# A three-layer network in one program: modulation through the attention, other banks, later norm rows, earlier decays

## The chip, the cores and the metric

One core of a Trainium2 chip runs the whole program. The metric is the device time of one execution, in microseconds (us). The kernel before was timed three times: the median is 1394.43 us, the lowest 1393.12 and the highest 1401.13. A further execution was recorded by the profiler.

## The reference, cut to what matters

The input is 256 tokens of width 1024, in float32. Two blocks follow each other. The first is a dilated window attention over three groups of eight heads, beside a pooling branch:

```python
h = rmsnorm(x, norm_g) * (1 + scale) + shift            # from c @ w_ada
q, k, v, z, u, ... = h @ w_in                           # 3 groups x 8 heads x 64
logits = q k^T / 8 + bias ; attn = softmax-merge of the 3 groups
merged = sigmoid(g_attn) * ((attn * silu(z_attn)) @ w_attn_br) \
       + sigmoid(g_pool) * ((pool(u) * silu(z_pool)) @ w_pool_br)
x = rmsnorm(x + gate * (merged @ w_out), final_g)
```

The second has two layers, on the 256 tokens `x` and on 256 context tokens `xc`. Each layer gets six vectors from `silu(c) @ w_mod` and six from `silu(c_ctx) @ w_mod`:

```python
sh1, sc1, g1, sh2, sc2, g2 = modulation(c, w_mod[i], b_mod[i])
h = x * (1 + sc1) + sh1                                 # the same for xc
y = mixer(h) @ w_out     # layer 0: retention (decay log1p(-exp(theta))) and gated linear
                         # attention (GLA), heads normalised; layer 1: window attention
x = layer_norm(alpha * x + g1 * y) * ln_g + ln_b
x = layer_norm(alpha * x + g2 * (relu(h2 @ w1)**2 @ w2)) * ln_g + ln_b
```

## The kernel before, in words

Every large product is made from float32 operands that are split into a rounded high part and the rest. `mm3` (L162) issues three matmuls for each tile: high by high, high by rest, rest by high. A weight tile of 512 KB is loaded by a DMA on SyncE's queue (`wload`, L135, four buffers `raw`), rounded by ScalarE (`whi`, L141) and subtracted by VectorE (`wlo`, L142). An activation is split in the same way by `split` (L108 to L111, tiles like `fx`).

PSUM has eight banks (L105): three named `mm` for the large products, two `S` for attention scores, two `T` for transposes, and one `O`. A tile that asks for a bank waits until the readers of its last holder are done.

The order of each engine's instructions is made when the program is built, by a scheduler that simulates the engines. `tc.issue_after(x)` holds back what is issued in it until the instruction x is placed. Each engine then runs its list strictly in order.

The first stage (0 to 54 us) makes the first block's shift and scale. Then come the products with `w_in` (54 to 217 us), the first block's attention (217 to 274), pooling and merging (274 to 360), `w_out` and the final norm (360 to 385), the modulation of the second block's first layer, `modulate` (L335), and the start of its products (385 to 405), retention (405 to 495), GLA (495 to 600), `proj_out` (600 to 655), the MLP of layer 0 (655 to 1030), window attention of layer 1 (1040 to 1175), its `proj_out`, and the MLP of layer 1 (to the end).

Fillers. The six modulation vectors of layer 0 need 24 MB of `w_mod`. A generator `quad` (L235) loads them 512 KB at a time on SyncE's queue (L257, tile `mvraw`, three buffers) and multiplies each with the two conditioning vectors (L251). All the products of one `quad` add into one tile in bank `O`, which it holds from its first step to its last. `fill(n)` steps the generators n times; `fill_behind` does so after each weight load of a large product, `rate[0]` steps at a time. Layer 1's vectors are made in the MLP of layer 0 by `summed` (L275), with the multiplications on VectorE (L292, tile `mva`).

Attention of the first block. `attention(h2)` (L549) treats two heads. For each of two query halves: scores on TensorE (L567, bank `S`); on VectorE the bias tile `B` is added and a row maximum taken (L570); exponent on ScalarE (L576), one over the sum and the scaling on VectorE (L577, L578); transposes on TensorE (L201, bank `T`), copies on ScalarE (L584). Then the products with v (L590), into bank `O`. The bias tiles are loaded by DMAs on GpSimd's queue (L554, two buffers). Ahead of the four head pairs `finish()` runs the generator that is under way to its end, so that bank `O` is free; no filler runs in the four head pairs.

Ends of stages. `modulate` transposes a normed row tile, scales and shifts it on ScalarE (`hf`, L346), rounds it (`hA`, L348) and subtracts (L349) on VectorE. Around it in program order stand the multiplication of the rows `xs` by `final_g` on GpSimd (L681) and the chain of small operations on 128x8 tiles that makes the decays from `ret_theta` (L684 to L705), with `W` (L720, L721) and `decs` (L726) made from it. `gla_out` (L921) makes the GLA output of one token tile in bank `O`; `head_norm` (L729) squares it on ScalarE (`hsq`, L733), sums on VectorE (L735), takes the root on GpSimd (`rs_y`, L206) and scales on VectorE (`yg`, L740). In the MLP, `late()` runs behind the split of the first hidden tiles (`g == 0`): `new_resid` (L996) multiplies the layer norm's output `r` by the gain and adds the bias, two VectorE operations for each of four row tiles (L997, L998), which gives the residual rows (`A1t` for the context, `xs` for the tokens).

Of the kernel before, what the change touches and what calls it, by code (L numbers as in the profile page):

```python
# [95 lines left out]
def body(tc, a, cst, out):  # L96
    nc = tc.nc
    with ExitStack() as ctx:
# [7 lines left out]
        def bank(tag):  # L106
            return psum.tile([P, 512], F32, tag=tag, name=tag, bufs={"mm": 3, "S": 2, "T": 2, "O": 1}[tag])
# [11 lines left out]

        def finish():  # L120

            if fillers and fillers[0].gi_running is False and fillers[0].gi_frame is not None and fillers[0].gi_frame.f_lasti > 0:
                for _ in fillers.pop(0):
                    pass
# [212 lines left out]
        def modulate(z, cols, dst, t0):  # L337

            A, B = cols
            for c in range(0, KC, 4):  # L340
                pt = bank("T")
                hf = tmp([P, 4, P], "hf")
                for i in range(4):
                    transpose(pt[:, i * P:(i + 1) * P], z[:, (c + i) * P:(c + i + 1) * P])
                for i in range(4):
                    nc.scalar.activation(hf[:, i, :], pt[:, i * P:(i + 1) * P], AF.Identity, scale=A[:, c + i:c + i + 1], bias=B[:, c + i:c + i + 1])  # L346
                hi, lo = (t[:, c:c + 4, t0:t0 + P] for t in dst)
                nc.vector.tensor_copy(hi, hf)  # L348
                nc.vector.tensor_sub(lo, hf, hi.bitcast(F32))  # L349
# [123 lines left out]

        nc.gpsimd.memset(relb[32:33, :], 1.0)
# [75 lines left out]
        def attention(h2):  # L550
# [6 lines left out]
            for qt in range(2):  # L557
# [4 lines left out]
                for g0, g1 in parts:  # L562
# [5 lines left out]
                    for e in range(2):  # L568
                        m = small.tile([P, 1], F32, tag="m", name="m")
                        nc.vector.tensor_tensor_reduce(out=prs[e][:, g0:g1, 0:nk], in0=sv[e], in1=Bs[e][:, g0:g1, 256 - nk:256], scale=-1.0,  # L570
                                                       scalar=3.0e38 if mins[e] is None else mins[e], op0=ALU.add, op1=ALU.min, accum_out=m)
                        mins[e] = m
                for e in range(2):
# [11 lines left out]
            o = bank("O")  # L585
# [12 lines left out]
        finish()  # L598
        for h2 in range(4):
            attention(h2)  # L600

# [78 lines left out]
        for t in range(2):  # L680
            nc.gpsimd.tensor_mul(xs[:, t, :], xs[:, t, :], fg)  # L681


        th = p2r.tile([P, 8], F32, tag="th", name="th")  # L684
        nc.gpsimd.dma_start(th, bcast_rows(a["ev_ret_theta_2"].rearrange("o d h -> o (d h)")))
        e_ = p2r.tile([P, 8], F32, tag="e_", name="e_")
        nc.scalar.activation(e_, th, AF.Exp)
        w_ = p2r.tile([P, 8], F32, tag="w_", name="w_")
        nc.vector.tensor_scalar(w_, e_, -1.0, 2.0, op0=ALU.mult, op1=ALU.add)
        nc.vector.reciprocal(w_, w_)  # L690
        nc.vector.tensor_mul(w_, w_, e_)
        w2 = p2r.tile([P, 8], F32, tag="w2", name="w2")
        nc.vector.tensor_mul(w2, w_, w_)
        ser = p2r.tile([P, 8], F32, tag="ser", name="ser")
        nc.vector.tensor_scalar(ser, w2, 1.0 / 13, 1.0 / 11, op0=ALU.mult, op1=ALU.add)
        for n in (9, 7, 5, 3, 1):
            nc.vector.tensor_mul(ser, ser, w2)
            nc.vector.tensor_scalar_add(ser, ser, 1.0 / n)
        nc.vector.tensor_mul(ser, ser, w_)
        nc.vector.tensor_scalar_mul(ser, ser, -2.0)  # L700
        ln_ = p2r.tile([P, 8], F32, tag="ln_", name="ln_")
        nc.scalar.activation(ln_, e_, AF.Ln, scale=-1.0, bias=1.0)
        big = p2r.tile([P, 8], F32, tag="big", name="big")
        nc.vector.tensor_single_scalar(big, e_, 0.25, op=ALU.is_gt)
        nc.vector.copy_predicated(ser, big.bitcast(U32), ln_)  # L705
# [12 lines left out]
        W = p2r.tile([P, 4, 384], F32, tag="W", name="W")  # L718
        for h in range(4):
            nc.vector.tensor_scalar_mul(W[:, h, :], dpn[:, 1, :], lgc[:, 4 + h:5 + h])  # L720
            nc.vector.scalar_tensor_tensor(W[:, h, :], dpn[:, 0, :], lgc[:, h:h + 1], W[:, h, :], op0=ALU.mult, op1=ALU.add)  # L721
        nc.scalar.activation(W, W, AF.Exp)
        decs = p2r.tile([P, 2, 8], F32, tag="decs", name="decs")
        for i in range(2):
            for d in range(2):
                nc.vector.tensor_scalar_mul(decs[:, i, 4 * d:4 * d + 4], lgc[:, 4 * d:4 * d + 4], sdec[:, i, d:d + 1])  # L726
# [194 lines left out]
        def gla_out(T):  # L921
            o = bank("O")
# [83 lines left out]
        def mlp(layer, Ts, xks, y, pool, mid, late, norm, after):  # L1006
# [4 lines left out]
            for g in range(8):  # L1011
# [24 lines left out]
                for i in range(0 if layer and g < 1 else 2):  # L1036
                    if g:
                        ws = w_a(w1, 512 * g + 256 * i)
                    for j in range(2):
# [8 lines left out]
                        split(fh[:, 2 * i + j, :], fl[:, 2 * i + j, :], f)  # L1048
                if g == 0:
                    with tc.issue_after(queued["split"]):  # L1050
                        late()
                    rate[0] = 2
# [53 lines left out]
        def late0():  # L1106
            for T in range(4):
                new_resid(T, r0[:, T, :], lnr)
# [151 lines left out]
        def late1():  # L1260
            for T in (2, 3):
                new_resid(T, r1[:, T, :], lnr1)
# [45 lines left out]
```

## Time and profile before

| | |
|---|---|
| median of three executions | 1394.43 us |
| profiled execution, its own time | 1394.03 us |
| its span, first to last instruction | 1392.2 us |
| TensorE (PE) busy | 1306.7 us, 94% |
| VectorE (DVE) busy | 823.2 us, 59% |
| ScalarE (ACT) busy | 575.3 us, 41% |
| GpSimd (POOL) busy | 90.7 us, 7% |
| mean DMA rate | 160 GB/s |

A group of instructions has its line in the program, the engine, what it writes and reads, and how many there are. The number in square brackets of a timeline row is the time that the engine was idle just before, and what ended that. PEclk is the clock that TensorE was granted: 1.00 is 2.4 GHz, 0.50 is 1.2 GHz, and a value between is a stretch with some of both. Matmul records are gathered in the timeline: "x4" is four records, and one `mvraw` tile of 512 KB leaves four.

### The profile page before, as it was taken

Reading aid. Unit: us, or ns where it says so; the run is one execution under the profiler, and the core shown is the slowest. Engines: PE = TensorE matmul, PEld = TensorE weight load, DVE = VectorE, ACT = ScalarE, POOL = GpSimd, SP = SyncE. Lnnn points to the kernel's source line nnn. Section 1 sums busy time; section 2 is a strip of 40 time slices with the busy share of each in tenths; the row PEclk is TensorE's granted clock in tenths of the full one; section 3 lists DMA queues with packets and bytes.
Section 4 is the critical chain, followed back from the end, with each engine's and each line's share of the span. In section 5 each row is a group of like instructions: output and inputs, shape, how many; then the busy total and the mean of one; then the engine's idle time right before and its main releaser. Section 6 shows DMA issues by size and latency. Waiting matters only on the chain.

```text
span 1392.2 us, 19721 instructions
## 1 busy us (share of the span) xinstructions
PE 1306.7 (94%) x7786; PEld 1058.7 (76%) x7786; DVE 823.2 (59%) x1318; ACT 575.3 (41%) x923; POOL 90.7 (7%) x144
## 2 busy tenths in 40 slices
PE   6999998899989999898799999999989898899995
PEld 5888864469887777677777777777769776698985
DVE  3534434436763447647676656663667888656566
ACT  2533323424552254323322332233345576465652
POOL 2010021000010300101000000000011000000000
PEclk9999998899999999989989999999999999899998
DMA  9898884375532141216354566553333504365661
GB/s 331 302 299 278 282 287 138 100 248 167 173 112 76 51 121 62 102 34 206 112 158 134 174 230 196 182 184 105 91 121 104 163 16 143 109 203 173 191 178 49
DMA packets 137988, 222.22 MB, mean 160 GB/s; under 512 B 8605, under 2 KB 86053, under 8 KB 137895
## 3 DMA queue, kind: packets, MB, share of 16 engines
q1 hardware_dynamic: 131984, 206.07, 46.5%
q0 software_dynamic: 5168, 14.34, 3.5%
q8 instruction: 61, 1.00, 0.3%
q10 hardware_dynamic: 742, 0.55, 0.1%
q14 instruction: 33, 0.26, 0.1%
HBM read 217.18 MB, written 1.13 MB: 157 GB/s over the span
## 4 chain that ended last, share of the span: by engine, by line
PE 84%; DVE 7%; DMA 3%; issue 2%; ACT 2%; POOL 0%; SPq 0%; DVEq 0%; ACTq 0%; POOLq 0%
PE mm L165 23%; PE mm L166 22%; PE mm L167 22%; PE O L251 3%; PE T L201 2%; PE mm L460 1%; DMA mvraw<-in_w_mod_dram 1%; DVE wlo L142 1%; PE O L1231 1%; DMA B<-tabd 1%; PE O L590 1%; PE O L429 1%; PE S L1206 1%; PE T L790 1%; DMA h1a<-in_w_ada_dram 1%
## 5 line engine op out<-in xcount | busy, mean ns | idle before, releaser
L142 DVE TENSOR_TENSOR wlo<-raw,whi 128x1024 fp32r<-128x1024 f32 x261 | 318.5, 1223 | 241.5 <-ACT whi L141 235.5
L141 ACT CAST whi<-raw 128x1024 fp32r<-128x1024 f32 x261 | 273.5, 1051 | 429.1 <-PE mm L167 227.3
L165 PE MATMUL mm<-whi,fx 128*128 128x512 f32 x384 | 155.2, 404 | 12.7 <-DVE y L1060 9.3
L166 PE MATMUL mm<-wlo,fx 128*128 128x512 f32 x384 | 152.9, 399 | 0.0
L167 PE MATMUL mm<-whi,fx 128*128 128x512 f32 x384 | 148.4, 400 | 0.0
L165 PEld LDWEIGHTS mm<-whi,fx 128*128 128x128 f32 x384 | 73.3, 191 | 36.8 <-DVE y L1060 9.7
L165 PE MATMUL mm<-A1a,whi 128*128 128x256 f32 x352 | 101.2, 288 | 0.0
L167 PE MATMUL mm<-A1a,wlo 128*128 128x256 f32 x352 | 99.6, 283 | 0.0
L166 PE MATMUL mm<-A1a,whi 128*128 128x256 f32 x352 | 99.4, 282 | 0.0
L166 PE MATMUL mm<-hBl,whi 128*128 128x512 f32 (+1 forms) x256 | 98.4, 385 | 0.0
L167 PEld LDWEIGHTS mm<-whi,fx 128*128 128x128 f32 x384 | 73.2, 191 | 17.3
L166 PEld LDWEIGHTS mm<-wlo,fx 128*128 128x128 f32 x384 | 73.3, 191 | 16.2
L165 PEld LDWEIGHTS mm<-A1a,whi 128*128 128x128 f32 x352 | 66.2, 188 | 15.2 <-issue 12.5
L292 DVE SCALAR_TENSOR_TENSOR mva<-mvraw,cst_m,mva 128x1024 f32<-128x1024 f32 x56 | 70.7, 1279 | 0.2
L1062 DVE TENSOR_TENSOR y<-y,mm 128x512 f32<-128x512 f32 x72 | 46.9, 682 | 37.4 <-PE mm L167 37.3
L167 PEld LDWEIGHTS mm<-A1a,wlo 128*128 128x128 f32 x352 | 66.3, 188 | 3.4 <-issue 3.4
L166 PEld LDWEIGHTS mm<-A1a,whi 128*128 128x128 f32 x352 | 66.3, 188 | 2.7 <-issue 2.7
L111 DVE TENSOR_TENSOR fx<-f,fx 128x512 fp32r<-128x512 f32 (+1 forms) x60 | 34.0, 566 | 56.2 <-ACT fx L110 56.0
L166 PE MATMUL mm<-hDl,whi 128*128 128x256 f32 x224 | 63.2, 282 | 0.0
L1046 ACT ACTIVATE f<-mm 128x512 f32<-128x512 f32 (+1 forms) x58 | 28.5, 491 | 78.3 <-PE mm L167 78.3
L166 PEld LDWEIGHTS mm<-hBl,whi 128*128 128x128 f32 x256 | 49.0, 192 | 10.4 <-issue 0.4
L165 PE MATMUL mm<-whi,hA 128*128 128x512 f32 x128 | 51.3, 401 | 0.0
(501 smaller groups left out, 2862.6 us busy)
## 6 DMA issues: line engine op xcount, KB each, us to landing
raw<-in_mlp_w_dram SPq DMA_DIRECT2D x128, 512.0 KB, 4.1
mvraw<-in_w_mod_dram SPq DMA_DIRECT2D x96, 512.0 KB, 5.0
raw<-in_w_in_dram SPq DMA_DIRECT2D x64, 512.0 KB, 6.6
raw<-in_ev_w_in_dram SPq DMA_DIRECT2D x25, 512.0 KB, 4.1
raw<-in_od_w_qkv_dram SPq DMA_DIRECT2D x12, 512.0 KB, 3.6
mvraw<-in_w_ada_dram SPq DMA_DIRECT2D x10, 512.0 KB, 7.3
raw<-in_w_out_dram SPq DMA_DIRECT2D x8, 512.0 KB, 3.9
raw<-in_ev_w_out_dram SPq DMA_DIRECT2D x8, 512.0 KB, 3.8
```

The costliest lines, as they stand in the source:

```text
L111: queued["split"] = nc.vector.tensor_sub(lo, src, hi.bitcast(F32)).ins
L141: nc.scalar.copy(hi, raw)
L142: queued["lo"] = nc.vector.tensor_sub(lo, raw, hi.bitcast(F32)).ins
L165: nc.tensor.matmul(o, lh, rh, start=first, stop=False)
L166: nc.tensor.matmul(o, lh, rl, start=False, stop=False)
L167: nc.tensor.matmul(o, ll, rh, start=False, stop=last)
L201: nc.tensor.transpose(o, i, ident[:n, :n])
L251: nc.tensor.matmul(acc[32 * j:32 * j + 32, :n], stat[:, k, :], raw[:, j * n % 1024:j * n % 1024 + n], start=k == 0, stop=k == KC - 1)
L292: nc.vector.scalar_tensor_tensor(acc, raw, stat[:, k, m:m + 1], acc, op0=ALU.mult, op1=ALU.add)
L429: nc.tensor.matmul(acc[32 * j:32 * j + 32, 0:P], cst_a[:, 4 * i + k, :], rs[j // 2][:, 256 * k + P * (j % 2):256 * k + P * (j % 2) + P], s ...
L1046: nc.scalar.activation(f, o, AF.Relu)
L1062: nc.vector.tensor_add(y[:, T, hs], y[:, T, hs], o)
```

## The change

Five things are done.

1. `finish()` goes away. Each query half of the first block's attention calls `fill(3)` behind its scores, eight times in all, so that the generators of layer 0's modulation go on there. Because a `quad` holds bank `O` meanwhile, the attention's output takes a bank `mm`. After the attention `rate[0]` is 1 where it was 2.
2. `gla_out` takes bank `O` for even and bank `S` for odd token tiles.
3. The chain of decays, with its DMA of `ret_theta` and its two table functions, is issued in the first stage.
4. `xs` times `final_g` goes from GpSimd to VectorE; it, `W` and `decs` are held back until the last subtraction of `modulate` is placed.
5. In the MLP of both layers, the layer norm's rows are only copied into the residual at `g == 0`, on ScalarE. The gain and the bias follow in place, one row tile for each of `g` 2 to 5 (layer 0) or 2 and 3 (layer 1).

```diff
--- before.py
+++ after.py
@@ -117,12 +117,6 @@
-        def finish():
-
-            if fillers and fillers[0].gi_running is False and fillers[0].gi_frame is not None and fillers[0].gi_frame.f_lasti > 0:
-                for _ in fillers.pop(0):
-                    pass
...
@@ -346,7 +340,7 @@
                 nc.vector.tensor_copy(hi, hf)
-                nc.vector.tensor_sub(lo, hf, hi.bitcast(F32))
+                queued["mod"] = nc.vector.tensor_sub(lo, hf, hi.bitcast(F32)).ins
...
@@ -469,6 +463,30 @@
+        th = const.tile([P, 8], F32, tag="th", name="th")
+        nc.gpsimd.dma_start(th, bcast_rows(a["ev_ret_theta_2"].rearrange("o d h -> o (d h)")))
+        e_ = const.tile([P, 8], F32, tag="e_", name="e_")
+        nc.scalar.activation(e_, th, AF.Exp)
...
+        for n in (9, 7, 5, 3, 1):
+            nc.vector.tensor_mul(ser, ser, w2)
+            nc.vector.tensor_scalar_add(ser, ser, 1.0 / n)
...
+        nc.scalar.activation(ln_, e_, AF.Ln, scale=-1.0, bias=1.0)
...
@@ -570,6 +588,7 @@
+                fill(3)
                 for e in range(2):
                     pv = prs[e][:, :, 0:nk]
...
@@ -582,7 +601,7 @@
-            o = bank("O")
+            o = bank("mm")
...
@@ -595,9 +614,9 @@
-        finish()
         for h2 in range(4):
             attention(h2)
+        rate[0] = 1
...
@@ -677,32 +696,9 @@
-        for t in range(2):
-            nc.gpsimd.tensor_mul(xs[:, t, :], xs[:, t, :], fg)
...
-        th = p2r.tile([P, 8], F32, tag="th", name="th")
...
-        nc.scalar.activation(e_, th, AF.Exp)
...
-        nc.vector.copy_predicated(ser, big.bitcast(U32), ln_)
+        with tc.issue_after(queued["mod"]):
+            for t in range(2):
+                nc.vector.tensor_mul(xs[:, t, :], xs[:, t, :], fg)
...
+        with tc.issue_after(queued["mod"]):
+            W = p2r.tile([P, 4, 384], F32, tag="W", name="W")
...
@@ -919,7 +916,7 @@
-            o = bank("O")
+            o = bank("OS"[T % 2])
...
@@ -1046,9 +1043,9 @@
+                with tc.issue_after(queued["split"]):
+                    late(g)
                 if g == 0:
-                    with tc.issue_after(queued["split"]):
-                        late()
                     rate[0] = 2
...
@@ -1103,9 +1100,12 @@
-        def late0():
-            for T in range(4):
-                new_resid(T, r0[:, T, :], lnr)
+        def late0(g):
+            for T in range(4) if g == 0 else [g - 2] if 1 < g < 6 else []:
+                if g:
+                    new_resid(T, resid(T), lnr)
+                else:
+                    nc.scalar.copy(resid(T), r0[:, T, :])
...
@@ -1257,9 +1257,12 @@
-        def late1():
-            for T in (2, 3):
-                new_resid(T, r1[:, T, :], lnr1)
+        def late1(g):
+            for T in (2, 3) if g == 0 else [g] if g in (2, 3) else []:
+                if g:
+                    new_resid(T, resid(T), lnr1)
+                else:
+                    nc.scalar.copy(resid(T), r1[:, T, :])
```

The lines of the changed program stand six lower from L117 on, and differ more further down. The scheduler makes these orders of it.

TensorE's list in the first block's attention, in the second head pair (`S` are scores, `T` transposes, `PT,A0a` the products with v). Before:

```order
L590 MATMUL O<-PT,A0a 64x256
L201 MATMUL T<-ident,pr 128x128 x3
L567 MATMUL S<-h1a 128x256 x2
L590 MATMUL O<-PT,A0a 64x256
L590 MATMUL O<-PT,A0a 64x128
L567 MATMUL S<-h1a 128x256 x2
L590 MATMUL O<-PT,A0a 64x128
L590 MATMUL O<-PT,A0a 64x256 x2
L590 MATMUL O<-PT,A0a 64x128 x2
L590 MATMUL O<-PT,A0a 64x256 x2
L590 MATMUL O<-PT,A0a 64x128 x2
```

Of the change, with the filler's products (`mvraw`, two matmuls for each 512 KB tile):

```order
L195 MATMUL T<-ident,pr 128x128 x6
L245 MATMUL O<-mvraw,cst_m 32x512 x2
L195 MATMUL T<-ident,pr 128x128 x3
L609 MATMUL mm<-PT,A0a 64x256
L245 MATMUL O<-mvraw,cst_m 32x512 x2
L195 MATMUL T<-ident,pr 128x128 x3
L609 MATMUL mm<-PT,A0a 64x256
L609 MATMUL mm<-PT,A0a 64x128
L245 MATMUL O<-mvraw,cst_m 32x512 x2
L609 MATMUL mm<-PT,A0a 64x128
L609 MATMUL mm<-PT,A0a 64x256 x2
```

In all, 28 such products now stand among the head pairs, about seven for each. The 144 triples of matmuls with `A1a` (the last products with `w_in`, for the gates), which stood between the first scores and the last filler ahead of the attention, now stand in its last head pair and behind it.

TensorE's list at the end of GLA, the outputs of the last two token tiles (`gqd`, `gsm`), the transposes of retention's rows `yr` and the first products of `proj_out` (`yH`). Before:

```order
L927 MATMUL O<-ST,gqd 64x128 x2
L167 MATMUL mm<-whi,hA_3290 128x512
L201 MATMUL T<-ident,yr 128x128 x8
L925 MATMUL O<-vx,gsm 128x128
L927 MATMUL O<-ST,gqd 64x128 x2
L925 MATMUL O<-vx,gsm 128x128
L927 MATMUL O<-ST,gqd 64x128 x2
L925 MATMUL O<-vx,gsm 128x128
L927 MATMUL O<-ST,gqd 64x128 x2
L925 MATMUL O<-vx,gsm 128x128
L927 MATMUL O<-ST,gqd 64x128 x2
L165 MATMUL mm<-whi,yH 128x512
```

Of the change:

```order
L924 MATMUL S<-ST,gqd 64x128 x2
L922 MATMUL S<-vx,gsm 128x128
L924 MATMUL S<-ST,gqd 64x128 x2
L924 MATMUL O<-ST,gqd 64x128 x2
L922 MATMUL O<-vx,gsm 128x128
L924 MATMUL O<-ST,gqd 64x128 x2
L922 MATMUL O<-vx,gsm 128x128
L195 MATMUL T<-ident,yr 128x128 x4
L924 MATMUL O<-ST,gqd 64x128 x2
L922 MATMUL O<-vx,gsm 128x128
L924 MATMUL O<-ST,gqd 64x128 x2
L159 MATMUL mm<-whi,yH 128x512
```

Both outputs now stand ahead of any wait for the norm of either, in two banks.

VectorE's list in the MLP of layer 0, behind the split of the first hidden tiles (`fx`); `mva` is `summed`, and `y` the copies that empty the banks `mm` of the first products with `w2`. Before:

```order
L142 TENSOR_TENSOR wlo<-raw,whi 128x1024
L292 SCALAR_TENSOR_TENSOR mva<-mvraw,cst_m,mva 128x1024
L111 TENSOR_TENSOR fx<-f,fx 128x512
L997 TENSOR_TENSOR A1t<-r_5258,lnr_5652 128x1024 x2
L997 TENSOR_TENSOR xs<-r_5258,lnr_5652 128x1024 x2
L292 SCALAR_TENSOR_TENSOR mva<-mvraw,cst_m,mva 128x1024
L998 TENSOR_TENSOR A1t<-A1t,lnr_5653 128x1024 x2
L998 TENSOR_TENSOR xs<-xs,lnr_5653 128x1024 x2
L1060 COPY y_5656<-mm 128x512 x3
L142 TENSOR_TENSOR wlo<-raw,whi 128x1024
```

Of the change:

```order
L111 TENSOR_TENSOR fx<-f,fx 128x512
L136 TENSOR_TENSOR wlo<-raw,whi 128x1024
L286 SCALAR_TENSOR_TENSOR mva<-mvraw,cst_m,mva 128x1024
L111 TENSOR_TENSOR fx<-f,fx 128x512
L286 SCALAR_TENSOR_TENSOR mva<-mvraw,cst_m,mva 128x1024
L1057 COPY y_5656<-mm 128x512 x3
L136 TENSOR_TENSOR wlo<-raw,whi 128x1024
```

The eight operations on `lnr` are gone from there and stand singly further down. The four copies that take their place are on ScalarE, and the scheduler places them ahead, in the end of `proj_out`: the two of `A1t` among the `whi` casts ahead of the first group of `hf`, one of `xs` between two `whi` casts ahead of the second group, and one just ahead of the last group of `hf`. In `modulate`'s stage the second scaling of `xs` (L650) now stands ahead of all four casts and subtractions of `hA`, and nothing else of VectorE stands between those.

## Rows read from the trace of the kernel before

**Rows 1.** The page: the span, and the chain that ended last by engine.

```profile
span 1392.2 us, 19721 instructions
...
PE 84%; DVE 7%; DMA 3%; issue 2%; ACT 2%; POOL 0%; SPq 0%; DVEq 0%; ACTq 0%; POOLq 0%
```

**Rows 2.** Busy time by stretch: start:end, length, PE, PEld, DVE, ACT, POOL; PEclk, DMA share, GB/s.

```profile
205.00:280.00 75.00, 62.62 (x330) 37.38 (x327) 33.43 (x96) 28.63 (x63) 7.87 (x11) 0.84 0.43 131
...
385.00:405.00 20.00, 15.34 (x105) 14.77 (x105) 16.61 (x43) 12.37 (x27) 4.75 (x2) 0.83 0.20 67
...
580.00:605.00 25.00, 19.61 (x95) 13.82 (x94) 11.69 (x22) 5.79 (x9) 4.23 (x4) 0.73 0.49 169
...
685.00:705.00 20.00, 10.70 (x35) 8.22 (x35) 17.10 (x17) 2.10 (x2) 0.00 (x0) 0.74 0.27 83
...
705.00:1205.00 500.00, 477.26 (x2496) 385.12 (x2495) 341.40 (x541) 215.40 (x376) 18.25 (x30) 0.98 0.45 143
```

**Rows 3.** What engines waited for: us in total, times, longest.

```profile
SPq L257 <- PE O L251: 92.7, 39, 11.4
...
PE mm L165 <- DVE y L1060: 9.3, 1, 9.3
...
PE O L251 <- DMA mvraw<-in_w_mod_dram: 5.6, 3, 3.1
...
DVE pr L570 <- DMA B<-tabd: 9.2, 5, 2.7
```

**Rows 4.** TensorE in the attention: start, us, instruction, idle before.

```profile
210.26 1.05 PE L251 MATMUL O<-mvraw,cst_m 128*32 128x512 f32 x4 [0.94 <-DMA mvraw<-in_w_mod_dram]
...
245.64 1.31 PE L567 MATMUL S<-h0a 64*128 64x256 f32 x4 [0.47 <-DVE m L570]
...
249.25 2.34 PE L201 MATMUL T<-ident,pr 128*128 128x128 f32 x9 [0.79 <-DVE den L577]
...
258.75 1.31 PE L567 MATMUL S<-h0a 64*128 64x256 f32 x4 [0.47 <-DVE m L570]
```

**Rows 5.** Tile `mvraw`: from issue to landing.

```profile
DMA to landing us min/median/max: 3.5/5.1/10.7
```

**Rows 6.** Tile `B`: from issue to landing.

```profile
DMA to landing us min/median/max: 4.9/5.4/9.4
```

**Rows 7.** VectorE in the stage of `modulate`.

```profile
387.94 2.82 DVE L349 TENSOR_TENSOR hA<-hf,hA 128x512 fp32r<-128x512 f32 x1
...
393.26 2.25 DVE L697 TENSOR_TENSOR ser<-ser,w 128x8 f32<-128x8 f32 x1
395.54 0.17 DVE L698 TENSOR_SCALAR ser<-ser 128x8 f32<-128x8 f32 x1
...
400.30 0.68 DVE L349 TENSOR_TENSOR hA<-hf,hA 128x512 fp32r<-128x512 f32 x1
```

**Rows 8.** GpSimd in the same stage.

```profile
387.80 2.41 POOL L681 TENSOR_TENSOR xs<-xs,fg 128x1024 f32<-128x1024 f32 x1 [3.00 <-DMA fg<-in_final_g_dram]
```

**Rows 9.** ScalarE in the same stage.

```profile
388.95 1.28 ACT L702 ACT_TABLE_LOAD   x1
...
392.66 2.90 ACT L346 ACTIVATE hf<-T,m,x0aA 128x128 f32<-128x128 f32 x8 [2.21 <-PE T L201]
```

**Rows 10.** TensorE at the end of GLA.

```profile
589.33 0.77 PE L925 MATMUL O<-vx,gsm 128*128 128x128 f32 x2 [4.21 <-DVE yg L740]
...
595.95 0.79 PE L165 MATMUL mm<-whi,yH 128*128 128x512 f32 x1 [1.17 <-ACT yH L957]
```

**Rows 11.** VectorE at the start of layer 0's MLP.

```profile
686.52 2.35 DVE L997 TENSOR_TENSOR A1t<-r,lnr 128x1024 f32<-128x1024 f32 x2
...
696.80 1.88 DVE L1060 COPY y<-mm 128x512 f32<-128x512 f32 x3
```

**Rows 12.** ScalarE ahead of that, in `proj_out`'s end.

```profile
642.19 1.05 ACT L141 CAST whi<-raw 128x1024 fp32r<-128x1024 f32 x1 [17.14 <-PE mm L167]
```

**Rows 13.** ScalarE in the first stage.

```profile
15.18 1.04 ACT L141 CAST whi<-raw 128x1024 fp32r<-128x1024 f32 x1 [7.29 <-DMA raw<-in_w_in_dram]
```

More of the change, by code (lines that the diff above doesn't have):

```diff
@@ L471, in body @@
             nc.vector.tensor_scalar_mul(cst_m[:, :, m], sg[:, m, :], 0.5)
+        th = const.tile([P, 8], F32, tag="th", name="th")
+        nc.gpsimd.dma_start(th, bcast_rows(a["ev_ret_theta_2"].rearrange("o d h -> o (d h)")))
+        e_ = const.tile([P, 8], F32, tag="e_", name="e_")
+        nc.scalar.activation(e_, th, AF.Exp)
+        w_ = const.tile([P, 8], F32, tag="w_", name="w_")
+        nc.vector.tensor_scalar(w_, e_, -1.0, 2.0, op0=ALU.mult, op1=ALU.add)
+        nc.vector.reciprocal(w_, w_)
+        nc.vector.tensor_mul(w_, w_, e_)
+        w2 = const.tile([P, 8], F32, tag="w2", name="w2")
+        nc.vector.tensor_mul(w2, w_, w_)
+        ser = const.tile([P, 8], F32, tag="ser", name="ser")
+        nc.vector.tensor_scalar(ser, w2, 1.0 / 13, 1.0 / 11, op0=ALU.mult, op1=ALU.add)
+        for n in (9, 7, 5, 3, 1):
+            nc.vector.tensor_mul(ser, ser, w2)
+            nc.vector.tensor_scalar_add(ser, ser, 1.0 / n)
+        nc.vector.tensor_mul(ser, ser, w_)
+        nc.vector.tensor_scalar_mul(ser, ser, -2.0)
+        ln_ = const.tile([P, 8], F32, tag="ln_", name="ln_")
+        nc.scalar.activation(ln_, e_, AF.Ln, scale=-1.0, bias=1.0)
+        big = const.tile([P, 8], F32, tag="big", name="big")
+        nc.vector.tensor_single_scalar(big, e_, 0.25, op=ALU.is_gt)
+        nc.vector.copy_predicated(ser, big.bitcast(U32), ln_)
         nc.gpsimd.memset(relb[32:33, :], 1.0)
@@ L679, in body @@
         nc.gpsimd.dma_start(fg, bcast_rows(a["final_g"]))
-        for t in range(2):
-            nc.gpsimd.tensor_mul(xs[:, t, :], xs[:, t, :], fg)
-        th = p2r.tile([P, 8], F32, tag="th", name="th")
-        nc.gpsimd.dma_start(th, bcast_rows(a["ev_ret_theta_2"].rearrange("o d h -> o (d h)")))
-        e_ = p2r.tile([P, 8], F32, tag="e_", name="e_")
-        nc.scalar.activation(e_, th, AF.Exp)
[L688 to L704, printed above, removed]
-        nc.vector.copy_predicated(ser, big.bitcast(U32), ln_)
+        with tc.issue_after(queued["mod"]):
+            for t in range(2):
+                nc.vector.tensor_mul(xs[:, t, :], xs[:, t, :], fg)
         dpn = p2r.tile([P, 2, 384], F32, tag="dpn", name="dpn")
@@ L717, in body @@
             nc.vector.tensor_copy(lgp[64 * e:64 * e + 64], lv[64 * e:64 * e + 64, :, :, e])
[L718 to L726, printed above, removed]
+        with tc.issue_after(queued["mod"]):
+            W = p2r.tile([P, 4, 384], F32, tag="W", name="W")
+            for h in range(4):
+                nc.vector.tensor_scalar_mul(W[:, h, :], dpn[:, 1, :], lgc[:, 4 + h:5 + h])
+                nc.vector.scalar_tensor_tensor(W[:, h, :], dpn[:, 0, :], lgc[:, h:h + 1], W[:, h, :], op0=ALU.mult, op1=ALU.add)
+            nc.scalar.activation(W, W, AF.Exp)
+            decs = p2r.tile([P, 2, 8], F32, tag="decs", name="decs")
+            for i in range(2):
+                for d in range(2):
+                    nc.vector.tensor_scalar_mul(decs[:, i, 4 * d:4 * d + 4], lgc[:, 4 * d:4 * d + 4], sdec[:, i, d:d + 1])
         nc.scalar.activation(decs, decs, AF.Exp)
```

## The prediction, made before the changed kernel was run

> **What bounds the kernel now.** I read the page first: TensorE carries 84% of the chain that ended last, in a span of 1392.2 us [rows 1]. The work of TensorE is hardly changed here, so what can be gained is of two kinds: time in which it stands still, and time in which it runs at half its clock behind such a stop. Both are read from the busy time by stretch [rows 2]: the length of a stretch less PE's busy time is the idle time, and the busy time by one less PEclk is about what the lower clock costs. Four stretches bear on the change:
>
> - attention of the first block, 205 to 280 us: 75.0 - 62.62 = 12.4 us idle, 62.62 x 0.16 = 10.0 us of clock, 22.4 in all
> - `modulate` and what follows, 385 to 405: 4.7 idle, 15.34 x 0.17 = 2.6 of clock, 7.3 in all
> - the end of GLA, 580 to 605: 5.4 idle, 19.61 x 0.27 = 5.3 of clock, 10.7 in all
> - the start of layer 0's MLP, 685 to 705: 9.3 idle, 10.70 x 0.26 = 2.8 of clock, 12.1 in all
>
> Then the waits say which releaser ends last in each [rows 3], and the timelines of these stretches show what stood ahead of that releaser on its own engine [rows 4, 7 to 13].
>
> **Part 1, fillers through the attention.** Before, the running generator is brought to its end ahead of the head pairs. Its products come faster than its tiles: TensorE waits 5.6 us in three waits for `mvraw` [rows 3], since a product takes about 1.05 us [rows 4] and a tile 5.1 us to land, with three buffers [rows 5]. Then the head pairs run alone: one begins at 245.64 and the next at 258.75, a period of 13.1 us, with 0.47 + 0.79 = 1.3 us idle in it [rows 4]; four make 5.0 us. After the change seven products stand in each pair: PE's work in a pair goes from 11.8 to 11.8 + 7 x 1.0 = 18.8 us, while the loop through VectorE and ScalarE, which closes in 13.1 us now, is no longer. So the idle time inside the pairs should shrink; I leave half, 2.5 us. The tiles are wanted every 18.8 / 7 = 2.7 us, and three buffers at the median landing give one every 1.7 us; only landings above 3 x 2.7 = 8.1 us are late, and the longest was 10.7 [rows 5]. I leave 2.5 us for those. The last pair's tail is covered by the 144 triples of `A1a` matmuls that now stand there. That makes 5 us of idle time where there were 12.4; the clock loss, which follows stops, I take down in nearly the same proportion, to 4.5. Gain: 22.4 - 9.5 = **13 us**. The upper bound is all, 22; the lower is a loss, which the rivals price.
>
> The attention's output in a bank `mm` costs nothing while the triples are held back behind it; if one of them needed that bank, the wait would be one output's life, 2 us or so by the rows of L201 and L567 around it [rows 4]. `rate[0] = 1` afterwards leaves few products for the merge stage, where PE was full; nothing.
>
> Against this part stands the bias tile. VectorE already waits 9.2 us for `B` in five waits [rows 3], though the fillers were stopped then; `B` lands in 5.4 us by the median and 9.4 at the longest [rows 6]. With the weight tiles under way it will land later. I count on the scheduler's earlier issue and on the 7 us of filler work in each pair to cover it. The Trainium skill ("DMA: Bandwidth & Descriptors", Queues, rings and completion order) speaks against me here: each DMA engine takes turns between the queues that have work, a packet at a time, so that `B` on GpSimd's queue shares the engines with `mvraw` on SyncE's. No row here shows the two together in the attention; by the rule the first rival's time, below, is the sum.
>
> **Part 2, `modulate`.** The last subtraction of `hA` ends at 400.98 [rows 7]. Ahead of it stand a subtraction of 2.82 us that takes 0.68 elsewhere, while GpSimd multiplies `xs` [rows 7, 8], and a 128x8 product of 2.25 us whose like takes 0.17, in GpSimd's second multiplication: 2.1 + 2.1 us. Between them lie some 18 operations of the decay chain, 3 us. And ScalarE's second group of `hf` began 2.2 us late, for transposes [rows 9] of rows whose scaling had stood behind the long subtraction. All of that is taken away, about 9 us on a path that cost 7.3. I take 6 and leave 1.3 for what is ScalarE's own, two groups of 2.9 us [rows 9]. Bounds 3 and 7.3. On the other side, the multiplications on VectorE cost two times 1.2 us, as operations of that size do [rows 11], behind the last subtraction, then `W`, then the next `wlo`; I take +1 (0 to +3), as PE has just got its four operands and works on the first of its weights.
>
> **Part 3, GLA.** The 4.21 us for `yg` is the wait for the one bank `O` [rows 10]. With two banks it goes. The 1.17 us for `yH` stays, and the norms of both tiles then come at once, ahead of the transposes of `yg`: next late, but behind some 24 matmuls. So 4.2 us and nearly half of the 5.3 us of clock: **6.5 us**. Bounds 3 (the norm chain is late by as much) and 10.
>
> **Part 4, the residual of layer 0.** Eight operations of 1.18 us, 9.4 us in all [rows 11], stood between the split and the copies of `y`, for which PE waited 9.3 us [rows 3]. They go. In their place are four ScalarE copies, priced at 1.05 us by the cast of that size [rows 12]: the first two lie in ScalarE's idle 17.14 us [rows 12], one lies in a busy stretch ahead of an `hf` and costs its 1.05, the last lies in a gap. One `mva` still stands ahead of the `y` copies; I leave 1 us for it. 12.1 - 2.1 = **10 us**, bounds 6 and 12. The same eight operations run later, 2.4 us for each of four hidden groups; VectorE is busy 341.4 of 500 us in that part [rows 2], so they fit; without the slack they would cost 9.4. In layer 1 the same edit counts nothing: no wait of PE for it is among the rows of that place.
>
> **Part 5, decays early.** ScalarE is idle for 7.29 us ahead of its first cast [rows 13], which is more than exponent, table load of 1.28 us [rows 9] and logarithm; twenty small VectorE operations of 0.17 us [rows 7] make 3.4 us. If `ret_theta` lands late they stand in front of the first cast: +0.5, bounds 0 and +2. Another table load later lies in a stage where ScalarE waits.
>
> **Sum.** -13 - 6 + 1 - 6.5 - 10 + 0.5 = -34 us, from the profiled 1394.03 us: **1360 us**. That execution is 0.4 us under the median of 1394.43, so nothing is to be corrected.
>
> **The rivals.**
>
> *The bias tile decides.* `B` lands at 9.4 us in place of 5.4 in three pairs (the first pair's is loaded long before); TensorE works in order, and 3 x 4 = 12 us of waiting eat part 1. For it: the waits for `B` now [rows 3]. Against it: 7 us of filler products in each pair. 1360 + 12 = 1372 us. Chance 0.20.
>
> *The stop moves.* In parts 2 to 4 the next operation is nearly as late (GLA's norms, ScalarE's `hf`, the `mva`), and half of 22.5 us stays: 1371 us. For it: 1.17 us at `yH` already [rows 10]. Against: the releasers named are gone from the order. Chance 0.11.
>
> *All comes back*, idle time and clock: 20 + 7 + 10 + 12 less 1.5, so 1346 us. For it: each stop costs clock behind it, so fewer stops pay twice. Chance 0.12.
>
> *Slower: TensorE stands in order behind `mvraw`.* Twenty-eight products now stand between scores and transposes, and a late tile holds up all behind it; SyncE's queue already waits 92.7 us for these buffers [rows 3]. At the longest landing, 10.7 us with three buffers, a tile comes every 3.6 us, and 28 take 100 us where the four pairs need 75. That is +25, the 13 of part 1 are gone, and another 10 of clock: 1360 + 48 = 1408 us. It decides from a mean wait of 34 / 28 = 1.2 us for each product. Against it: the median landing is less than half of that. Chance 0.05.
>
> That the change doesn't do what it says is excluded by the instruction lists, but for layer 1, where I expect nothing.
>
> **How the numbers follow.** The forecast, 1352 to 1368 by the bounds of its parts, has 0.52. The range takes in the two rivals around 1372 and the one at 1346, and their own spread of a few us: 1345 to 1377. About 1% (13.9 us) is what a measurement of this kernel tells from no change; faster is below 1380.5 us. The forecast and the three rivals below that hold 0.95; I take 0.88 faster, since several of their terms could fail together, 0.09 within 1%, and 0.03 slower, half of the last rival with a little of its like.
>
> **What would show it.** In the changed profile PE's busy time in the head pairs near their length, waits of TensorE for `mvraw` under 5 us in sum and of VectorE for `B` not above 10; no wait of PE for `yg` of 4 us and none for `y` of 9; the four subtractions of `hA` at 0.7 us each. The prediction is wrong if PE's waits for `mvraw` or for `pr` in the attention exceed 15 us, or if PEclk there stays at 0.84.

## The result, and the profile after

The changed kernel takes 1352.7 us (median of four executions, 1352.12 to 1356.32) against 1393.9 us (1393.12 to 1401.13). The ratio is 0.9699, with a 95% interval of 0.9662 to 0.9735. The forecast was 1360 us, range 1345 to 1377. The profiled execution took 1356.32 us, so its span, 1354.5 us against 1392.2, understates the gain by 3.5 us.

The stages are compared between marks that both programs have: the first product with `cst_m` (layer 0's modulation), the first with `mg` (`w_out`), the first with `yH` (`proj_out` of layer 0), the first and last with `hBh` (layer 0's MLP). Lengths from the two traces, in us:

| stretch | before | after | difference | my terms |
|---|---|---|---|---|
| start to `cst_m` | 107.2 | 108.3 | +1.1 | +0.5 |
| `cst_m` to `mg`: attention | 247.8 | 232.6 | -15.2 | -13 |
| `mg` to `yH`: `modulate`, retention, GLA | 241.0 | 228.5 | -12.5 | -6 + 1 - 6.5 |
| `yH` to first `hBh` | 57.5 | 57.2 | -0.3 | 0 |
| first to last `hBh`: MLP 0 | 357.0 | 344.8 | -12.2 | -10 |
| to the end | 381.7 | 383.1 | +1.4 | 0 |
| sum | 1392.2 | 1354.5 | -37.7 | -34 |

The busy time of the changed kernel by stretch, with the columns of [rows 2]. The first two stretches are its attention. The last three are the places of parts 2 to 4, as long as in [rows 2] and as far from the marks (the first products with `mg`, `yH` and `hBh`).

```profile
175.00:205.00 30.00, 27.50 (x149) 12.03 (x149) 15.50 (x45) 11.01 (x24) 10.03 (x15) 0.89 0.81 242
205.00:262.00 57.00, 50.29 (x287) 25.55 (x286) 18.48 (x56) 17.96 (x41) 5.54 (x9) 0.91 0.63 196
...
371.00:391.00 20.00, 19.90 (x160) 19.03 (x159) 14.20 (x27) 13.31 (x28) 0.00 (x0) 1.00 0.30 89
553.40:578.40 25.00, 23.34 (x149) 17.90 (x148) 19.38 (x42) 10.06 (x15) 3.17 (x4) 0.93 0.48 169
658.10:678.10 20.00, 19.69 (x85) 15.66 (x84) 16.73 (x19) 4.21 (x4) 0.00 (x0) 1.00 0.59 173
```

In the places of parts 2 to 4, 0.1, 1.7 and 0.3 us are idle, at PEclk 1.00, 0.93 and 1.00, where [rows 2] had 4.7, 5.4 and 9.3 us at 0.83, 0.73 and 0.74. The attention is not cured: 2.5 + 6.7 = 9.2 us are still idle there and PEclk is 0.89 and 0.91.

What the engines of the changed kernel wait for, to be set beside [rows 3]: us in total, times, longest.

```profile
PE O L245 <- DMA mvraw<-in_w_mod_dram: 8.7, 6, 2.2
...
PE mm L159 <- ACT yH L954: 1.7, 1, 1.7
...
PE mm L159 <- DVE y L1057: 0.3, 1, 0.3
...
DVE pr L588 <- DMA B<-tabd: 10.3, 2, 5.8
```

The 9.3 us for `y` are now 0.3, and the 4.2 us for `yg` [rows 10] are gone. What is left in these places is `yH` (1.7 us, 1.17 before), `mvraw`, more than before, and `B`.

VectorE in `modulate`, answering to [rows 7]: the subtractions take 0.69 us, and `xs` times `final_g` follows the last of them.

```profile
373.90 0.69 DVE L343 TENSOR_TENSOR hA<-hf,hA 128x512 fp32r<-128x512 f32 x1
...
380.45 0.69 DVE L343 TENSOR_TENSOR hA<-hf,hA 128x512 fp32r<-128x512 f32 x1
381.06 2.35 DVE L701 TENSOR_TENSOR xs<-xs,fg 128x1024 f32<-128x1024 f32 x2
```

TensorE at the end of GLA, answering to [rows 10]: the last output, then only the wait for `yH`, behind which the clock falls once more.

```profile
567.27 0.44 PE L924 MATMUL O<-ST,gqd 128*64 128x128 f32 x4
569.38 0.80 PE L159 MATMUL mm<-whi,yH 128*128 128x512 f32 x1 [1.66 <-ACT yH L954]
```

VectorE at the start of the MLP, answering to [rows 11]: one `mva` between the split and the copies of `y`.

```profile
658.40 0.69 DVE L111 TENSOR_TENSOR fx<-f,fx 128x512 fp32r<-128x512 f32 x1
659.00 1.28 DVE L286 SCALAR_TENSOR_TENSOR mva<-mvraw,cst_m,mva 128x1024 f32<-128x1024 f32 x1
660.30 1.89 DVE L1057 COPY y<-mm 128x512 f32<-128x512 f32 x3
```

And three rows of three engines in the second head pair of the changed kernel: GpSimd issues the two loads of `B` at 204.55, VectorE has waited 5.82 us for them when it goes on at 213.00, and TensorE stands 2.18 us in front of a tile.

```profile
204.55 1.54 POOL L572 DMA_DIRECT2D B<-tabd  x2 [13.15 <-DVE m L588]
```

```profile
213.00 0.56 DVE L588 CUSTOM_DVE_ANT_1 pr<-S,B 128x384 f32<-128x384 f32 x1 [5.82 <-DMA B<-tabd]
```

```profile
210.09 1.18 PE L245 MATMUL O<-mvraw,cst_m 128*32 128x512 f32 x4 [2.18 <-DMA mvraw<-in_w_mod_dram]
```

### The profile page after: what moved, and what is told of

The parts are those of the page before. It is cut to its first block, busy times and chain, and to the rows that moved or that the text cites. A ratio compares the mean times of both kernels' runs of the same rounds, so it can differ in the third digit from the quotient of the medians.

```text
span 1354.5 us, 19733 instructions
## 1 busy us (share of the span) xinstructions
PE 1286.2 (95%) x7786; PEld 1046.9 (77%) x7786; DVE 820.9 (61%) x1320; ACT 582.0 (43%) x929; POOL 85.4 (6%) x142
## 4 chain that ended last, share of the span: by engine, by line
PE 45%; DVE 5%; ACT 2%; issue 1%; DMA 1%; DVEq 0%; ACTq 0%
PE mm L159 14%; PE mm L160 13%; PE mm L161 13%; PE T L195 1%; PE O L1231 1%; DVE wlo L136 1%; PE S L1206 1%; ACT whi L135 1%; ACT hf L340 1%; DVE y L1059 1%; DMA A1t<-A1t 0%; DVE pr L1213 0%; PE O L292 0%; DVE mva L286 0%; DVE tm L974 0%
## 5 line engine op out<-in xcount | busy, mean ns | idle before, releaser
L160 PEld LDWEIGHTS mm<-hBl,whi 128*128 128x128 f32 x256 | 49.0, 191 | 10.2 <-issue 0.4
```

What stands on the lines that cost most here:

```text
L160: nc.tensor.matmul(o, lh, rl, start=False, stop=False)
```

## The experiments

Ratios are to the kernel before, timed beside each. Since the parts are worth 0.6 to 1.5 per cent each, the length of the part's own stretch in the profiled execution says more than the ratio; it is that of one execution.

**The parts alone.** Each is the kernel before with one part of the diff and nothing else.

Part 1 (`finish` out, `fill(3)`, bank `mm`, rate 1):

> Part 1 alone (no finish, fill(3) in the head pairs, the attention's output in a bank mm, rate 1 behind it); parts 2 to 5 as before. Between the first product with cst_a and the first product with mg the trace of the whole change is 15.2 us shorter than that of before. Theory 'terms add' (each part gains its own stage's idle time, clock and little else): 1394 - 15 = 1379 us, ratio 0.989, and the stages behind 355 us keep their lengths. Rival 'shared' (the early decays and the freed GpSimd help the attention too, or part 1 pays for others): a ratio above 0.992 or below 0.986.

Measured: 1378.4 us against 1398.04, ratio 0.985 (0.9827 to 0.9873); `cst_m` to `mg` 232.4 us, as with the whole change. The stages behind keep their lengths (`mg` to `yH` 240.4, MLP 356.8). So in the traces the terms add. The ratio, though, is past 0.986, where I had put the rival 'shared'. Its interval reaches to both sides of that bound, and the kernel before was slower beside this one than beside the whole change (1398.04 us against 1393.9), so the ratio decides nothing here; the stretches do.

Parts 2 and 5:

> Parts 2 and 5 alone (decay chain in the first stage, xs*final_g on VectorE behind the last subtraction, W and decs behind it). From the first product with mg to the last with hA the trace of the whole change is 5.7 us shorter, and its first stage 1.1 us longer. 'Terms add': 1394 - 4.6 = 1389.4 us, ratio 0.9967. Rival 'the place moves the wait': the stage is shorter but W comes late and the retention behind it gives it back, ratio 0.999 or above.

Measured: 1389.85 against 1398.04, ratio 0.9937 (0.9914 to 0.996); `mg` to the last `hA` 222.8 us against 228.7, and nothing given back behind it (to `yH` 12.2 against 12.3). The first mark is at 108.7.

Part 3:

> Part 3 alone (gla_out in bank O for even, S for odd tiles). From the last product with hA to the first with yH the trace of the whole change is 6.8 us shorter. 'Terms add': 1394 - 6.8 = 1387 us, ratio 0.995. Rival: the bank S is wanted by the scores of gla_tile, whose wait takes half of it back: 0.9975 or above.

Measured: 1389.66 against 1398.04, ratio 0.9935 (0.9912 to 0.9957); `mg` to `yH` 233.4 us against 241.0, 7.6 shorter. The rival falls.

Part 4:

> Part 4 alone (residual copied on ScalarE, gain and bias later). From the first product with hBh to the last the trace of the whole change is 12.2 us shorter, with nothing given back later. 'Terms add': 1394 - 12.2 = 1382 us, ratio 0.991; the four alone then sum to 15 + 4.6 + 6.8 + 12.2 = 38.6 us against 37.7 in the two profiles. My own term was 10 us, which would be 0.9928.

Measured: 1385.8 against 1398.04, ratio 0.99 (0.9875 to 0.9925); the MLP 343.7 us against 357.0, 13.3 shorter.

The four gains on their own stretches are 15.4, 6.0 (`mg` to `yH`, 235.0), 7.6 and 13.3 us; the first stage's mark swings by 1 us or more from one execution to the next. They add to 42.3, where the whole change has 15.2 + 12.5 + 12.2 = 39.9 us on the same three stretches. By the medians they would add to 48.5, against the slower kernel before, where the whole change gained 41.2. So the parts add in the main, and a few us between these sums are not explained part by part.

The executions of these kernels without part 1 also show something that no single profile could: `cst_m` to `mg`, which is the same code in all of them (TensorE's order differs in a few places), took 247.8 (before), 246.2 (parts 2 and 5), 250.6 (part 3) and 254.2 us (part 4), and 245.9 and 249.6 in two kernels further down, while the two with part 1 took 232.6 and 232.4. The kernel before, and then the kernel with part 4 alone, in the stretch in which they differ most:

```profile
215.00:230.00 15.00, 13.52 (x65) 8.97 (x63) 6.74 (x22) 6.02 (x14) 4.65 (x7) 0.66 0.50 147
230.00:275.00 45.00, 39.05 (x211) 23.03 (x207) 22.97 (x72) 20.45 (x47) 3.22 (x4) 0.85 0.25 69
```

```profile
215.00:230.00 15.00, 14.62 (x53) 9.48 (x55) 6.62 (x23) 6.03 (x14) 4.66 (x7) 0.50 0.52 153
230.00:275.00 45.00, 36.86 (x179) 22.79 (x179) 18.77 (x61) 17.76 (x42) 3.23 (x4) 0.77 0.22 59
```

Same instructions, and the clock stayed at its lower level for longer after the stop ahead of the head pairs. The executions of the kernel before, timed beside these, spread from 1394.55 to 1404.31 us, those with part 1 from 1377.15 to 1379.35, which fits; but a kernel with part 1 further down spreads over 8.5 us, so part 1 does not end the swing for good. Of the six traces without part 1, the 247.8 us that I read is the third shortest.

For the stretch from `cst_m` to `mg` the traces give TensorE's idle time and, in the records of the granted clock, the time at its lower level. Since that level is half of the upper one, half of this time is the most that it can have cost; the last column takes it and the idle time off the length. All in us:

| kernel | length | idle | lower clock | length less idle and half of that |
|---|---|---|---|---|
| before | 247.8 | 12.4 | 23.9 | 223.4 |
| parts 2 and 5 | 246.2 | 14.4 | 13.7 | 225.0 |
| part 4 | 254.2 | 13.5 | 37.5 | 222.0 |
| part 1 | 232.4 | 10.8 | 13.7 | 214.8 |
| the whole change | 232.6 | 9.2 | 17.1 | 214.8 |

Two things can be read here. The swing between the kernels without part 1 is for the most part the clock's. And part 1 gains 7 to 10 us that are neither idle time nor clock: the kernel with part 1 alone has as much time at the lower clock as the one with parts 2 and 5, and is 13.8 us shorter, of which 3.6 are idle time. The two as views, parts 2 and 5 first:

```profile
108.70:354.90 246.20, 231.81 (x1589) 175.11 (x1589) 108.99 (x187) 90.50 (x134) 18.58 (x28) 0.97 0.68 216
```

```profile
106.90:339.30 232.40, 221.62 (x1589) 170.17 (x1589) 108.00 (x187) 89.53 (x133) 18.36 (x28) 0.97 0.73 229
```

**What part 1 consists of.** Variants of the whole change. Without the fillers in the pairs:

```diff
-                fill(3)
...
-        rate[0] = 1
+        rate[0] = 2
```

> The whole change without fill(3) in the head pairs, and rate 2 behind the attention as in the kernel before; no finish, output in a bank mm as in the change. The list of TensorE still has products among the first head pairs (issued earlier), none in the last two, and the rest in the merge. Stretch from the first product with cst_m to the first with mg: 232.6 us with the change, 247.8 before. Theory 'cover' (products fill the pairs' waits): about half of the pairs have their waits back, 2.5 us idle and as much of clock: 237 to 239 us, ratio to before 0.973 to 0.975. Rival 'only the stop ahead of the pairs counted': 232 to 233 us, ratio 0.970.

Measured: 1359.18 against 1395.16, ratio 0.9729 (0.9712 to 0.9747); `cst_m` to `mg` 238.7 us. This is as 'cover' had it. Against the 247.8 us of the trace before, about 9 of the 15 us are there without the fill calls, with no stop ahead of the pairs and only the products that were issued earlier, and 6 come from the products that the calls put into the pairs (the rate behind the attention, 1 or 2, goes with them). The waits of `pr`, `den` and `m` that the products cover are back, while `mvraw` has one left:

```profile
PE S L585 <- DVE m L588: 3.3, 4, 1.0
PE O L245 <- DMA mvraw<-in_w_mod_dram: 2.4, 1, 2.4
PE T L195 <- ACT pr L594: 1.7, 1, 1.7
PE T L195 <- DVE den L595: 1.5, 2, 0.8
```

Fewer and more fillers, `fill(2)` and `fill(4)`:

> The whole change with fill(2): 16 steps in the attention in place of 24, the rest in the merge behind it. 'mvraw decides': the tiles are wanted every 4 us in place of 2.7, TensorE's waits for mvraw fall from 8.7 to 5 us or less and the stretch from cst_m to mg gets 2 to 4 us shorter, 229 to 231 us. 'Cover' (every product more in the pairs gains): 3 us longer, 235 to 236.

> The whole change with fill(4): up to 32 steps in the attention. 'mvraw decides': tiles wanted every 2 us, which three buffers at a landing of 4.9 us can just give alone, but not beside B: waits for mvraw 12 us or more, the stretch from cst_m to mg 3 to 6 us longer, 236 to 238 us. 'Cover': 231 us or less.

Measured: with two 1350.71 us, ratio 0.9675 (0.966 to 0.969), stretch 228.2 us; with four 1366.09, ratio 0.9782 (0.9762 to 0.9803), stretch 242.6 us. Between two, three and four the order is as 'mvraw decides' has it. But with two the waits for `mvraw` only fell to 7.5 us and TensorE's idle time from `cst_m` to `mg` not at all (9.5 us against 9.2); what fell is its time at the lower clock, 10.2 us against 17.1. So why two beat three is not shown. With four, 15.1 us are idle, and TensorE's waits are:

```profile
PE O L245 <- DMA mvraw<-in_w_mod_dram: 13.7, 7, 3.6
```

A third buffer for the bias tile:

```diff
-                B = p1t.tile([P, 3, 256], F32, tag="B", name="B", bufs=2)
+                B = p1t.tile([P, 3, 256], F32, tag="B", name="B", bufs=3)
```

> The whole change with three buffers for the bias tile B in place of two, so that one of the next pair's two loads can start a pair earlier. In the change VectorE waits 10.3 us for B in two waits, but TensorE's only waits in the pairs are 8.7 us for mvraw. Theory 'mvraw decides': the waits for B shrink by half or more and the stretch from cst_m to mg stays at 232.6 us, within 1. Rival 'the bias tile decides': 3 us or more shorter, 229 us or less.

Measured: 1348.71 us, ratio 0.9662 (0.9647 to 0.9676), stretch 225.4 us, 7.2 shorter. My theory falls, and the rival's number is met: no row of TensorE names `B`, and yet the stretch gets shorter. VectorE has no wait for `B` left, and TensorE waits for `mvraw` less than half as long:

```profile
PE O L245 <- DMA mvraw<-in_w_mod_dram: 4.0, 3, 1.8
PE T L195 <- DVE pr L597: 0.3, 1, 0.3
```

PEclk is 0.94 and 0.97 in the two stretches of the attention, where the change has 0.89 and 0.91. But the third buffer also led the scheduler to another order: 25 products of the filler stand among the head pairs, where the change has 28. So it is not shown that the earlier landing of `B` alone makes the 7.2 us. Against `B` as the only limit stands `fill(4)`, where VectorE waits only 4.9 us for it and the stretch is the longest of these variants.

The same loads issued by ScalarE in place of GpSimd (`nc.scalar.dma_start(B, ...)`):

> The whole change with the loads of the bias tile issued on ScalarE's queue in place of GpSimd's (two buffers as in the change). B lands in 8.1 us in the change, 5.4 before. Theory 'the DMA engines are shared': B still lands in 7 to 8.5 us, the stretch from cst_m to mg stays at 232 to 233 us. Rival 'GpSimd's queue is what is slow': B lands in 6 us or less, VectorE's 10.3 us for B halve, and the stretch gets 3 us shorter or more.

Measured: 1349.12 us, ratio 0.9667 (0.9634 to 0.9699), stretch 224.5 us, 8.1 shorter. Neither theory is met as a whole: `B` lands between them,

```profile
DMA to landing us min/median/max: 5.9/6.6/9.0
```

VectorE still waits 11.3 us for it, in five waits of at most 3.6 us in place of two of up to 5.8, and the stretch is shorter all the same. Here too 25 products stand among the pairs. How much is the queue's and how much the scheduler's other order, these runs can't tell apart.

Both of the better versions, three buffers and `fill(2)`:

> The whole change with three buffers for B and fill(2), the two versions that beat it put together. If both took away the same waiting, the stretch from cst_m to mg is that of three buffers alone, 225 to 226 us, ratio 0.966; if they add, 221 to 222 us, ratio 0.963. If 'cover' is now short (16 products in place of 24 with B no longer late), 228 us.

Measured: 1346.36 us (1342.01 to 1350.56) against 1395.02, ratio 0.9653 (0.9607 to 0.9699), stretch 222.4 us. They add nearly. It is the fastest kernel here by its median, though its interval meets that of the change; by its own stretch it is 10.2 us shorter.

**What part 2 consists of.** The kernel before, with only `xs` times `final_g` moved to VectorE, behind the last subtraction; and with only the decay chain moved to the first stage.

> The kernel before with one edit: xs*final_g on VectorE behind the last subtraction of hA; the decay chain stays where it was. Stretch from the first product with mg to the last with hA: 228.7 us before, 222.8 with parts 2 and 5. Theory 'GpSimd holds VectorE': the subtraction of 2.82 us and the product of 2.25 us fall to 0.7 and 0.2, which is 4.2 of the 5.9 us: 224 to 225. Rival 'the chain of small operations decides': 227 or more.

> The kernel before with the decay chain (and its two table functions) moved to the first stage, xs*final_g on GpSimd as before. 'GpSimd holds VectorE': the long subtraction stays, and the first rows' chain with it; 18 operations of 0.17 us go, 2 to 3 us: 226 to 227. Rival: 224 or less. First stage: 1.1 us longer in the change; the same here if the chain is the cause (first product with cst_m at 108.3 against 107.2), 107.2 if it isn't.

Measured: the first 1390.93 us against 1395.02, ratio 0.9959 (0.9935 to 0.9984), `mg` to the last `hA` 223.8 us; the second 1398.19, ratio 1.0025 (1.0005 to 1.0045), 229.6 us, and its first mark at 110.6. VectorE with the multiplication moved and the chain still in place: the subtraction is short and the second scaling follows.

```profile
385.66 0.69 DVE L349 TENSOR_TENSOR hA<-hf,hA 128x512 fp32r<-128x512 f32 x1
386.27 0.75 DVE L650 TENSOR_SCALAR xs<-xs,rs_y 128x1024 f32<-128x1024 f32 x1
```

VectorE with the chain moved and the multiplication still on GpSimd: `W` and `decs`, whose inputs are ready early now, slip between the casts, and one of them is held up in the place of the subtraction.

```profile
394.10 2.45 DVE L721 TENSOR_SCALAR W<-dpn,ser 128x384 f32<-128x384 f32 x4 [1.00 <-DMA dpn<-cst_dpn_dram]
396.47 0.68 DVE L349 TENSOR_TENSOR hA<-hf,hA 128x512 fp32r<-128x512 f32 x1
397.07 2.65 DVE L727 TENSOR_SCALAR decs<-ser,sdec 128x4 f32<-128x4 f32 x3
```

So 4.9 of the 5.9 us are the multiplication's (the kernels that leave this stage alone have 228.0 to 228.7 us); the early decays by themselves are worth nothing or a little less, and pay only with `W` and `decs` held back. The Trainium skill ("SBUF — State Buffer", Who interferes with whom) has VectorE and GpSimd share one pair of ports under an exclusive lock, for which a VectorE instruction with two inputs in SBUF contends with a GpSimd instruction that reads SBUF. The rows agree: the subtraction, which has two inputs, took 2.82 us beside 2.41 us of GpSimd [rows 7, 8] and 0.69 us here.

## Why the prediction was right, point by point

The sum was -34 us, and the traces gave -37.7, the medians -41.2. For parts 2 to 4 the reckoning of idle time and clock held within 1.5 us: what [rows 2] had less what is left is 7.2, 7.4 and 11.8 us, and the stretches got 6.0, 7.6 and 13.3 us shorter in the runs with one part. For part 1 it did not, and that its size came out is luck.

**Part 1, -13, measured -15.2 in the two traces, and 13 to 22 us against the traces of the other kernels without it.** The size came out, but not by the working. I left 5 us of idle time and 4.5 of clock; 9.2 us are idle, and 27.50 x 0.11 + 50.29 x 0.09 = 7.6 are the clock's. By my own reckoning that would have been a gain of 22.4 - 9.2 - 7.6 = 5.6 us. The step that failed is the ceiling: idle time and clock are not all that can be gained. TensorE's busy time from the first filler product with `cst_a` to the first with `mg` fell as well, with the same instructions, from 120.15 + 30.00 + 60.12 + 77.50 = 287.8 us to 119.10 + 27.50 + 50.29 + 78.90 = 275.8 us, of which the clock explains 2 to 3. A part of it can be read. TensorE before, at 190 us: the starts of the triples' matmuls lie 0.12 us apart, but 0.21 ahead of a filler product and 0.22 behind it.

```profile
189.98 0.28 PE L165 MATMUL mm<-A1a,whi 128*128 128x256 f32 x1
190.10 0.28 PE L166 MATMUL mm<-A1a,whi 128*128 128x256 f32 x1
190.31 1.05 PE L251 MATMUL O<-mvraw,cst_m 128*32 128x512 f32 x4
191.30 0.39 PE L167 MATMUL mm<-A1a,wlo 128*128 128x256 f32 x1
191.52 0.28 PE L165 MATMUL mm<-A1a,whi 128*128 128x256 f32 x1
191.64 0.28 PE L166 MATMUL mm<-A1a,whi 128*128 128x256 f32 x1
```

In the order before, 29 groups of filler products stand so, between two rows of triples; after, 10. At 0.2 us each, 19 fewer make some 4 us, an estimate. The traces bear it out: from start to start, idle time taken off, the triples from `cst_m` to `mg` take 142.7 to 142.9 us in the six kernels without part 1, 139.7 in the change and 139.8 with part 1 alone. By the same count the filler products keep their 39 us, and the attention's own matmuls (scores, transposes, products with v) go from 47.8 to 41.2 us. This is where most of the rest lies, the clock's share with it. Why they are shorter beyond that is not shown, and 5 to 7 us stay open.

The `A1a` work that moved into the last pair and behind it is 144 matmuls, which is 48 triples and not 144 as I had it; it covers a third of what I counted on there.

**The bias tile** was my rival with 0.20, and it was half right: `B` lands in 8.1 us in place of 5.4, VectorE waits 10.3 us for it, and the third buffer, with the order that comes with it, takes 7.2 us off. It came true beside a gain that was larger than I thought, not in place of it. My sign for it (VectorE's waits for `B` not above 10 us) was passed at 10.3, as was the one for `mvraw` (5 us, and it was 8.7). The sentence of the Trainium skill ("DMA: Bandwidth & Descriptors", Queues, rings and completion order) that I set against myself, that the DMA engines take turns between queues, agrees with this in so far as `B` lands later the more of `mvraw` is under way beside it: in 5.5 us without the fill calls, 7.2 with two and 8.1 with three. That the engines take turns no row shows.

**The tiles.** Three buffers at the median landing were to be enough. With `fill(4)` they are not (13.7 us of waits, 10 us longer). At three steps I left 2.5 us of waits and 8.7 were paid. That `fill(2)` is 4.4 us shorter is not due to these waits, which fell by 1.2.

**Part 2, -6 and +1, measured -5.9** alone, and the +1 was not paid (`mg` to `yH` is 6.0 us shorter). The reading of the two long VectorE operations as GpSimd's doing was right; the count of 18 small operations as 3 us of the path was not: taken away beside it they bring 1.0 us (222.8 against 223.8).

**Part 3, -6.5, measured -7.6** alone. The wait for `yH` stayed and grew, from 1.17 to 1.66 us, and behind it the clock still falls: 23.34 x 0.07 = 1.6 us of clock are left where there were 5.3. So 3.7 of the clock's 5.3 us went, more than the half that I took.

**Part 4, -10, measured -12.2 and 13.3 alone.** The 1 us for the `mva` was not paid: TensorE waits 0.3 us for `y`. The 1 us for a copy ahead of `hf` shows in TensorE's longest wait for `hf`, at the end of `proj_out`, but not in the length of that stretch (`yH` to the first `hBh` 57.2 us against 57.5, and 57.7 with part 4 alone). TensorE's waits for `hf` before, and then in the change:

```profile
PE T L201 <- ACT hf L346: 3.4, 2, 2.6
```

```profile
PE T L195 <- ACT hf L340: 3.9, 2, 3.6
```

Here is the copy, between two casts of ScalarE:

```profile
619.09 2.02 ACT L135 CAST whi<-raw 128x1024 fp32r<-128x1024 f32 x2
620.98 1.08 ACT L1108 COPY xs<-r 128x1024 f32<-128x1024 f32 x1
621.93 1.08 ACT L135 CAST whi<-raw 128x1024 fp32r<-128x1024 f32 x1
```

The eight postponed operations cost nothing where they went, as was said: the rest of the MLP keeps its length.

**Part 5, +0.5, measured +1.1, unclear.** `ret_theta` is there at 9.92 us and its table load is done well ahead of the first cast, which waits for its weights. The first mark lies between 106.8 and 110.6 us in all these executions, with and without the chain, so 1 us can't be told.

```profile
9.92 0.21 ACT L471 ACTIVATE e__627<-th 128x8 f32<-128x8 f32 x1 [2.04 <-DMA th<-in_ev_ret_theta_dram]
10.14 1.28 ACT L486 ACT_TABLE_LOAD   x1
...
16.91 2.17 ACT L135 CAST whi<-raw 128x1024 fp32r<-128x1024 f32 x2 [5.26 <-DMA raw<-in_w_in_dram]
```

**The other rivals.** *The stop moves* did not come: in the places of parts 2 to 4 TensorE has 2.1 us idle in place of 19.4. *All comes back*, 1346 us, came true in those places and not in the attention; 1352.7 us lies halfway between it and the forecast. The slower rival (TensorE in order behind `mvraw`) would have needed a mean wait of 1.2 us per product; it was 8.7 / 28 = 0.3 us, and with `fill(4)`, which goes that way, 0.4.

## What to carry to other kernels

A stop of TensorE costs its own length and then the lower clock behind it, and that second part differs from run to run (13.7 to 37.5 us at the lower clock in the attention of the kernels without part 1): price a stop from several executions, not from one. Idle time and clock are not a ceiling: here 7 to 10 us came beside them, of which 3 are read from the order in which matmuls of different kinds stand. Fill the waits of a latency-bound stage with independent work, but count what this work loads: here two steps a query half beat three and four lose, and a tile that becomes late (`B`) need not be one that TensorE's waits name. When work is moved earlier, hold back what depends on it, or the scheduler will put that in the gap.

## What the runs showed of the hardware that I had not expected

In the kernels without part 1 the same instructions from `cst_m` to `mg` took 245.9 to 254.2 us in six traces, with 13.7 to 37.5 us at the lower clock; with part 1 they took 232.4 and 232.6 in two. And a filler product that stands singly between triples of another kind of matmul spreads the starts of its neighbours from 0.12 to some 0.21 us on both sides; with fewer such places the triples of this stretch took 139.7 us in place of 142.8.
